# Low-rank products of a recurrence on half of the array each: a two-layer transformer block on one Trainium2 core

## The chip, the cores and the metric

The kernel runs on one core of a Trainium2 chip. The metric is the device time of one execution in microseconds (us), and the comparison is the median of several executions of each kernel. The core's engines have queues of their own and run in order: PE (TensorE, matmuls; PEld is its weight load), DVE (VectorE), ACT (ScalarE), POOL (GpSimd) and SP (SyncE, which issues most transfers).

## The reference

The function computes two layers on 256 tokens of width 2048 in fp32. The change touches the recurrence of the first layer, an RWKV-7 time mix with 16 heads of 64, of which this is the part that matters here (`heads` splits 1024 columns into heads; the scan and the norm behind it are left out):

```python
def rwkv7_time_mix(p_r, p_k, p_v, p_wd, p_ad, ...):
    ...
    wd = token_shift_lerp(p_wd, f(mu_w))          # 64 wide
    ad = token_shift_lerp(p_ad, f(mu_a))          # 64 wide
    w = -jax.nn.softplus(-(f(w0) + jnp.tanh(wd) @ f(w2))) - 0.5
    decay = jnp.exp(-jnp.exp(w))
    a = jax.nn.sigmoid(f(a0) + ad @ f(a2))
    kk = heads(k * f(k_k))
    kk = kk * lax.rsqrt(jnp.maximum(jnp.sum(kk * kk, axis=-1, keepdims=True), 1e-24))
    k = k * (1.0 + (a - 1.0) * f(k_a))
    ...
    o = rwkv7_scan(rh, dh, kh, vh, -kk, kk * ah)
```

The two low-rank products are `tanh(wd) @ w2`, for the decay, and `ad @ a2`, for the gate `a`. Each contracts over 64.

## The kernel before

Activations are held as 128 rows by tokens. Every large weight arrives in pieces of 128x1024 (SP), is cut into a rounded part `wh` by ACT (L171) and a rest `wl` by DVE (L179) or, for 7 pieces in 10 of the recurrence's stage, by POOL in four quarters (L177), and goes through PE as pairs of matmuls into a bank `g` of PSUM (three of them): 512 columns with `wh`, 256 with `wl`. Such a product is evicted by ACT (`et`, L220) and DVE (`z`, L223).

The recurrence runs in eight pairs of heads. For pair p there are three steps. `rwkv_inputs(p)` makes k, r and v by three large products, then the decay and the gate by the low-rank products, from these `kk`, `k`, and the tiles `atrt`, `bt_d`, `kt_d` that everything after it reads; `k`, `r`, `v`, `s`, `a`, `kk`, `bt_d`, `kt_d` and `t0` (the low-rank weights first, then the square of kk, which the matmul into `pk` sums) have one buffer each, so the next pair's inputs wait until this pair's are used up. `rwkv_inverse(p)` reads them by twelve matmuls into `G` (L593 to L595), and inverts a triangular matrix by five rounds of `Z` and `D`, each a matmul, a DVE instruction and the next matmul. `rwkv_chain(p)` walks over four chunks: a matmul, a copy by DVE (`X`), a matmul, a copy (`U`), a matmul, the new state by DVE (`S`), and so on; these matmuls write `ch` and `oT`.

The loop over p writes chain(p), inverse(p+1), inputs(p+2) and then fillers: group products of attention (`A0` to `A5`), gates, attention heads, and gate products of the merge that are made ahead and put into DRAM (L745). The order in which each engine gets its instructions is not that of the source: a scheduler sets it when the program is built, from its own estimate of times, and keeps it fixed. It may only move what the buffers allow. PSUM has eight banks in this stage: three for `g`, one for the tag `s` (pl, pk, ptk, sc of the attention over tokens), two for the tag `z` (G, Z and D of the inverse, among others), one for `ch` and one for `oT`. A tile of a tag gets the next bank of that tag in the order of the source, and has to wait until the tile that had it before is used up.

Behind the last pair, `raw` is cut into `yhl` (24 times an ACT cast, L234, and a DVE subtraction, L235), and `merge` reads it.

The lines that the change touches are in `rwkv_inputs`: `lora` holds tanh(wd) in rows 0 to 63 and ad in rows 64 to 127; `w2` is a tile whose columns 0 to 127 hold w2 in rows 0 to 63 and zeros below, and whose columns 128 to 255 hold zeros above and a2 in rows 64 to 127. Both products contract over all 128 rows and write the two halves of one bank, `pl`, of the tag `s`.

Of the kernel before, what the change touches and what calls it, by code (L numbers as in the profile page):

```python
# [11 lines left out]
AF = mybir.ActivationFunctionType  # L12
# [88 lines left out]
def _body(tc, a, out):  # L101
    nc = tc.nc
# [26 lines left out]
    def P(n, j=0, w=1):  # L129
        o, _ = _P[n]  # L130
        return par[:, o + j:o + j + w]

    def C(n, j=0, w=None):
        o, ww = _C[n]
        return con[:, o + j:o + j + (ww - j if w is None else w)]
# [10 lines left out]
    def ps_small(name, tag="s"):  # L146
        return psp.get(tag, psp["s"]).tile([128, 512], F32, tag=tag if tag in psp else "s", name=name)
# [4 lines left out]
    def mm(dst, lhsT, rhs, start=True, stop=True):  # L152
        nc.tensor.matmul(dst, lhsT=lhsT, rhs=rhs, start=start, stop=stop)  # L153
# [28 lines left out]
    def gemm_B(wd, act, kt=KD, m=128):  # L182

        ps = psg.tile([128, 512], F32, tag="g", name="g")
        for k0, kn in (chunks(kt) if m == 128 else [(0, kt)]):
            src = wd[128 * k0 * m:128 * (k0 + kn) * m].rearrange("(p c) -> p c", p=128)
            wh, wl = wchunk(src, kn * m)
            for j in range(kn):
                k = k0 + j
                mm(ps[:m, :], wh[:, j * m:(j + 1) * m], act[:, k, :], start=(k == 0), stop=False)  # L190
                mm(ps[:m, 256:512], wl[:, j * m:(j + 1) * m], act[:, k, 0:256], start=False, stop=(k == kt - 1))
        return ps
# [25 lines left out]
    def evict(ps, m=128, rstd=None, out=None, name="z"):  # L218
        t = scr.tile([128, 256], F32, tag="et", name="et", bufs=2)
        nc.scalar.copy(t[:m], ps[:m, 256:512])  # L220
        if rstd is None:
            z = out if out is not None else scr.tile([128, 256], F32, tag="ez", name=name, bufs=3)
            nc.vector.tensor_add(z[:m], ps[:m, 0:256], t[:m])  # L223
            return z
        nc.vector.tensor_add(t[:m], ps[:m, 0:256], t[:m])
        z = out if out is not None else scr.tile([128, 256], F32, tag="ez", name=name, bufs=3)
        nc.vector.tensor_mul(z[:m], t[:m], rstd[:m])
        return z
# [25 lines left out]
    def rsqrt(u, y):  # L254

        nc.scalar.activation(y, u, AF.Sqrt)
        nc.vector.reciprocal(y, y)  # L257
        newton(u, y)
# [82 lines left out]
    if True:  # L341
# [80 lines left out]
        hw0 = const.tile([128, 16], F32, tag="hw0", name="hw0")  # L422
        nc.vector.tensor_scalar(hw0, P("w0", 0, 16), 0.5, None, op0=ALU.mult)

        def shift(dst, z, mu):

            t = rw.tile([128, 256], F32, tag="tA", name="tA")
            nc.vector.tensor_sub(t, z[:, 0:256], z[:, 1:257])
            nc.vector.scalar_tensor_tensor(dst, t, mu, z[:, 1:257], op0=ALU.mult, op1=ALU.add)
# [59 lines left out]
        def raw_tile(ps):  # L489
            z = rw.tile([128, 257], F32, tag="zr", name="zr", bufs=2)  # L490
            nc.gpsimd.memset(z[:, 0:1], 0.0)
            evict(ps, out=z[:, 1:257])
            return z

        zw = raw_tile(gemm_B(a["w1B"][0], xg))
        lora = rw.tile([128, 256], F32, tag="lora", name="lora")
# [14 lines left out]
        def c4(t):  # L511
            return t.rearrange("p (c t) -> p c t", c=4)

        def diag(dst, off, fn):
            for h in range(2):
                s = slice(64 * h, 64 * h + 64)
                fn(dst[s, :, off + 64 * h:off + 64 * h + 64], s)

        def tmp(tag, bufs=1, shape=(128, 256), dt=F32):
            return rw.tile(list(shape), dt, tag=tag, name=tag, bufs=bufs)  # L520
# [3 lines left out]
        def rwkv_inputs(p):  # L524

            k = tmp("k")
            shift(k, raw_tile(gemm_B(a["w1B"][1 + p], xg)), P("mu_k", p))
            r = tmp("r")
            shift(r, raw_tile(gemm_B(a["w1B"][9 + p], xg)), P("mu_r", p))
            v = tmp("v")  # L530
            shift(v, raw_tile(gemm_B(a["w1B"][17 + p], xg)), P("mu_v", p))
            w2 = tmp("t0")
            nc.sync.dma_start(w2, a["lora2"][p])
            pl = ps_small("pl")
            mm(pl[:, 0:256], w2[:, 0:128], lora)
            mm(pl[:, 256:512], w2[:, 128:256], lora)
            s = tmp("s")
            nc.scalar.activation(s, pl[:, 0:256], AF.Tanh, bias=hw0[:, p:p + 1], scale=0.5)
            av_ = tmp("a")
            nc.scalar.activation(av_, pl[:, 256:512], AF.Tanh, bias=hw0[:, 8 + p:9 + p], scale=0.5)  # L540
            nc.vector.tensor_scalar(s, s, 0.5, 0.5, op0=ALU.mult, op1=ALU.add)
            nc.vector.tensor_scalar(av_, av_, 0.5, 0.5, op0=ALU.mult, op1=ALU.add)
            cum = tmp("cum")
            nc.vector.tensor_tensor_scan(cum, C("scan"), s, 0.0, op0=ALU.mult, op1=ALU.add)
            nc.gpsimd.tensor_sub(s, cum, s)
            e1 = s
            nc.scalar.activation(e1, s, AF.Exp, scale=-DECAY_C)
            ep = tmp("ep", 2)
            nc.scalar.activation(ep, cum, AF.Exp, scale=-DECAY_C)
            en = cum  # L550
            nc.scalar.activation(en, cum, AF.Exp, scale=DECAY_C)

            kk = tmp("kk")
            nc.vector.tensor_scalar(kk, k, P("k_k", p), None, op0=ALU.mult)
            t0 = tmp("t0")
            nc.scalar.activation(t0, kk, AF.Square)
            pk = ps_small("pk")
            mm(pk[:, 0:256], bdones, t0)
            nc.vector.tensor_scalar(t0, pk[:, 0:256], 1e-24, None, op0=ALU.max)
            rsqrt(t0, tmp("tA"))  # L560
            nc.vector.tensor_mul(kk, kk, t0)

            nc.vector.tensor_scalar(t0, av_, -1.0, P("k_a", p), op0=ALU.add, op1=ALU.mult)
            nc.vector.scalar_tensor_tensor(k, t0, 1.0, k, op0=ALU.add, op1=ALU.mult)

            nc.vector.scalar_tensor_tensor(t0, r, P("r_k", p), k, op0=ALU.mult, op1=ALU.mult)
            mm(pk[:, 256:512], bdones, t0)
            nc.vector.tensor_mul(raw[:, 8 + p, :], v, pk[:, 256:512])

            atrt = atrt_b[p % 2]  # L570
            diag(atrt, 64, lambda d, sl: nc.vector.scalar_tensor_tensor(
                d, c4(kk)[sl], -1.0, c4(e1)[sl], op0=ALU.mult, op1=ALU.mult))
            nc.vector.tensor_mul(atrt[:, :, 0:64], c4(r), c4(ep))
            nc.gpsimd.tensor_mul(kk, kk, av_)
            diag(bt_d, 0, lambda d, sl: nc.vector.tensor_mul(d, c4(kk)[sl], c4(en)[sl]))
            diag(kt_d, 0, lambda d, sl: nc.vector.tensor_mul(d, c4(k)[sl], c4(en)[sl]))
            diag(v_d, 0, lambda d, sl: nc.gpsimd.tensor_copy(d, c4(v)[sl]))

            pair[p] = dict(atrt=atrt, ep=ep)
# [206 lines left out]
        def filler(p):  # L786
            for f in fillers[p]:
# [6 lines left out]
                else:  # L794
                    (group_A if f[0] == "A" else attention_A)(int(f[1]))

        rwkv_inputs(0)
        group_C()
        rwkv_inverse(0)
        attention_C_prep()  # L800
        attention_C(0)
        attention_C(1)
        rwkv_inputs(1)
        ahead(0)
        ahead(1)
        for p in range(8):
            rwkv_chain(p)
            if p == 0:
                attention_C(2)
                attention_C(3)  # L810

                r16b = r16p.tile([128, 4096], F32, tag="r16", name="r16b")
                aqk = r16b[:, 0:2048].rearrange("p (i t f) -> p i t f", i=2, t=2)
                tok_b.append(r16b[:, 2048:3584].rearrange("p (i c f) -> p i c f", i=3, c=4))
            if p < 7:
                rwkv_inverse(p + 1)
            if p < 6:
                rwkv_inputs(p + 2)
            filler(p)
# [94 lines left out]
    for i in range(8):  # L914
        z = evict(gemm_B(a["w2B"][i], xg2), rstd=rs_bc)
# [8 lines left out]
    for h in range(4):  # L924
# [7 lines left out]
        z = evict(gemm_B(a["w2B"][8 + h], xg2), rstd=rs_bc)  # L932
        nc.vector.scalar_tensor_tensor(qi, z, 128.0 ** -0.5, eq, op0=ALU.mult, op1=ALU.mult)
        ki = atp.tile([128, 256], F32, tag="ki", name="ki")
        z = evict(gemm_B(a["w2B"][12 + h], xg2), rstd=rs_bc)
# [10 lines left out]
        pa = ps_small("pa")  # L946
# [88 lines left out]
    for f in range(KF):  # L1035
        z = evict(gemm_B(a["w_gate"][f], xg3), rstd=rs_bc)
# [9 lines left out]
    p = ps_small("fin")  # L1046
# [92 lines left out]
```

## Time and profile before

| | us |
|---|---|
| median of 3 executions | 2959.39 |
| lowest and highest | 2958.73, 2959.72 |
| the profiled execution | 2959.55 |
| its span, first to last instruction | 2957.8 |
| PE busy in the span | 2919.8 |
| DVE busy | 1917.6 |
| ACT busy | 1452.8 |
| POOL busy | 645.9 |

A view by windows gives, for each stretch of the span, the busy time of each engine with the number of its instructions, and the share of TensorE's full clock that was granted (PEclk: 1.00 is 2.4 GHz, 0.50 is 1.2 GHz). A timeline row gives the start, the time, the engine, the line and the tiles, with the idle time of the engine ahead of it in brackets and who ended it. Matmuls overlap, so what one costs in a stream is the distance of starts, not its time. An fp32 matmul stands as two instructions in the trace.

### The profile page before, as it was taken

Reading aid. Unit: us, or ns where it says so; the run is one execution under the profiler, and the core shown is the slowest. Engines: PE = TensorE matmul, PEld = TensorE weight load, DVE = VectorE, ACT = ScalarE, POOL = GpSimd, SP = SyncE. Lnnn points to the kernel's source line nnn. Section 1 sums busy time; section 2 is a strip of 40 time slices with the busy share of each in tenths; the row PEclk is TensorE's granted clock in tenths of the full one; section 3 lists DMA queues with packets and bytes.
Section 4 is the critical chain, followed back from the end, with each engine's and each line's share of the span. In section 5 each row is a group of like instructions: output and inputs, shape, how many; then the busy total and the mean of one; then the engine's idle time right before and its main releaser. Section 6 shows DMA issues by size and latency. Waiting matters only on the chain.

```text
span 2957.8 us, 44491 instructions
## 1 busy us (share of the span) xinstructions
PE 2919.8 (99%) x16696; PEld 2567.0 (87%) x16696; DVE 1917.6 (65%) x3088; ACT 1452.8 (49%) x2201; POOL 645.9 (22%) x878
## 2 busy tenths in 40 slices
PE   9999999999999999999999999999999999999997
PEld 7888888889988888888888888888888888888886
DVE  6655776677637655657767766666667666666554
ACT  6443454445446554545454454454555444444443
POOL 0685577767683100100000000000000000000000
PEclk9999999999999999999999999999999999999999
DMA  7553344444456655655455555555555555555664
GB/s 285 181 173 104 109 133 144 141 137 134 132 171 206 208 190 192 210 179 178 143 174 170 191 191 188 191 191 188 191 186 192 190 189 191 191 188 188 189 189 146
DMA packets 150392, 522.45 MB, mean 177 GB/s; under 512 B 17104, under 2 KB 22480, under 8 KB 150176
## 3 DMA queue, kind: packets, MB, share of 16 engines
q1 hardware_dynamic: 147920, 513.47, 53.1%
q0 software_dynamic: 1824, 4.98, 0.4%
q8 instruction: 131, 2.15, 0.3%
q10 hardware_dynamic: 432, 1.15, 0.1%
q14 instruction: 85, 0.70, 0.1%
HBM read 514.56 MB, written 4.98 MB: 176 GB/s over the span
## 4 chain that ended last, share of the span: by engine, by line
PE 94%; DVE 4%; ACT 1%; POOL 1%; issue 0%; DMA 0%; DVEq 0%; SPq 0%; ACTq 0%; POOLq 0%
PE g L153 87%; PE D L153 1%; PE ch L153 1%; PE Z L153 1%; PE oT L153 1%; PE sc L153 1%; PE G L153 1%; PE po L153 1%; POOL wl L177 0%; DVE wl L179 0%; PE ptk L150 0%; PE glo L153 0%; PE pt L150 0%; PE pl L153 0%; DVE tA L257 0%
## 5 line engine op out<-in xcount | busy, mean ns | idle before, releaser
L153 PE MATMUL g<-xg,wh 128*128 128x512 f32 x4640 | 1633.7, 393 | 0.5 <-DVE z L223 0.5
L171 ACT CAST wh<-w 128x1024 fp32r<-128x1024 f32 (+1 forms) x962 | 1002.3, 1042 | 1253.9 <-PE g L153 760.2
L179 DVE TENSOR_TENSOR wl<-w,wh 128x1024 fp32r<-128x1024 f32 (+1 forms) x801 | 977.1, 1220 | 712.7 <-ACT wh L171 711.6
L153 PE MATMUL g<-xg,wl 128*128 128x256 f32 x4640 | 1317.8, 284 | 4.9 <-POOL wl L177 4.6
L153 PEld LDWEIGHTS g<-xg,wh 128*128 128x128 f32 x4640 | 871.0, 188 | 178.2 <-DVE z L223 0.7
L153 PEld LDWEIGHTS g<-xg,wl 128*128 128x128 f32 x4640 | 876.4, 189 | 7.5 <-POOL wl L177 4.9
L177 POOL TENSOR_TENSOR wl<-w,wh 128x256 fp32r<-128x256 f32 x644 | 494.9, 801 | 164.0 <-ACT wh L171 149.4
L153 PE MATMUL g<-yhl,wh 128*128 128x512 f32 x768 | 269.7, 390 | 0.0
L153 PE MATMUL g<-act,wh 128*128 128x512 f32 x704 | 244.2, 390 | 0.0
L153 PE MATMUL g<-wh,xg 128*128 128x512 f32 x768 | 243.7, 401 | 0.4 <-ACT va L357 0.4
L153 PE MATMUL g<-yhl,wl 128*128 128x256 f32 x768 | 216.6, 282 | 0.0
L153 PE MATMUL g<-act,wl 128*128 128x256 f32 x704 | 198.7, 282 | 0.0
L848 POOL TENSOR_TENSOR accm<-accm,z 128x256 f32<-128x256 f32 x64 | 53.4, 834 | 651.0 <-DVE z L847 651.0
L153 PEld LDWEIGHTS g<-yhl,wh 128*128 128x128 f32 x768 | 144.2, 188 | 30.4 <-ACT wh L171 0.3
L153 PEld LDWEIGHTS g<-wh,xg 128*128 128x128 f32 x768 | 142.4, 188 | 31.0 <-ACT va L357 0.5
L220 ACT COPY et<-g 128x256 f32<-128x256 f32 (+1 forms) x434 | 157.2, 362 | 6.9 <-PE g L153 6.9
L153 PEld LDWEIGHTS g<-act,wh 128*128 128x128 f32 x704 | 132.2, 188 | 27.7
L153 PE MATMUL g<-wl,xg 128*128 128x512 f32 x384 | 149.8, 404 | 0.2 <-DVE wl L179 0.2
L153 PEld LDWEIGHTS g<-yhl,wl 128*128 128x128 f32 x768 | 145.1, 189 | 0.0
L153 PEld LDWEIGHTS g<-act,wl 128*128 128x128 f32 x704 | 133.1, 189 | 0.0
L223 DVE TENSOR_TENSOR z<-g,et 128x256 f32<-128x256 f32 x216 | 90.3, 418 | 31.4 <-ACT et L220 31.1
L1010 POOL MEMSET cu<- 128x2 f32 x8 | 0.8, 102 | 415.1 <-DVE co L1017 350.3
(369 smaller groups left out, 2950.0 us busy)
## 6 DMA issues: line engine op xcount, KB each, us to landing
w<-w2B SPq DMA_DIRECT2D x208, 512.0 KB, 3.3
w<-w1B SPq DMA_DIRECT2D x194, 512.0 KB, 3.4
w<-w_gate SPq DMA_DIRECT2D x88, 512.0 KB, 3.3
w<-w_ffup SPq DMA_DIRECT2D x88, 512.0 KB, 3.3
w<-w1A SPq DMA_DIRECT2D x64, 512.0 KB, 3.3
w<-w_down SPq DMA_DIRECT2D x64, 448.0 KB, 3.3
w<-w_o SPq DMA_DIRECT2D x32, 512.0 KB, 4.3
w<-w2A SPq DMA_DIRECT2D x32, 512.0 KB, 3.4
```

Of the source, the lines that this page charges most:

```text
L153: nc.tensor.matmul(dst, lhsT=lhsT, rhs=rhs, start=start, stop=stop)
L171: nc.scalar.copy(wh[:, :nel], w[:, :nel])
L177: nc.gpsimd.tensor_sub(wl[:, sl], w[:, sl], wh[:, sl].bitcast(F32))
L179: nc.vector.tensor_sub(wl[:, :nel], w[:, :nel], wh[:, :nel].bitcast(F32))
L220: nc.scalar.copy(t[:m], ps[:m, 256:512])
L223: nc.vector.tensor_add(z[:m], ps[:m, 0:256], t[:m])
L848: nc.gpsimd.tensor_add(accm, accm, u)
L1010: nc.gpsimd.memset(cu[:, 0:2], 0.0)
```

## The change

The first product reads rows 0 to 63 of the weights and of `lora`, the second rows 64 to 127; the zeros are not read any more. In the built program the first has the place (0, 0) in an array of 64 rows by 128 columns, the second (64, 0). The second writes a bank of its own, `pa`, and that comes from the tag `z`, so it takes its turn among the tiles of the inverse. ACT reads the gate from there. All else in the source is as it was, and since the scheduler runs anew on it, the order of all engines differs from there to the first products of the merge.

```diff
@@ -531,13 +531,14 @@
             shift(v, raw_tile(gemm_B(a["w1B"][17 + p], xg)), P("mu_v", p))
             w2 = tmp("t0")
             nc.sync.dma_start(w2, a["lora2"][p])
-            pl = ps_small("pl")
-            mm(pl[:, 0:256], w2[:, 0:128], lora)
-            mm(pl[:, 256:512], w2[:, 128:256], lora)
+
+            pl, pa = ps_small("pl"), ps_small("pa", "z")
+            mm(pl[:, 0:256], w2[0:64, 0:128], lora[0:64, :])
+            mm(pa[:, 0:256], w2[64:128, 128:256], lora[64:128, :])
             s = tmp("s")
             nc.scalar.activation(s, pl[:, 0:256], AF.Tanh, bias=hw0[:, p:p + 1], scale=0.5)
             av_ = tmp("a")
-            nc.scalar.activation(av_, pl[:, 256:512], AF.Tanh, bias=hw0[:, 8 + p:9 + p], scale=0.5)
+            nc.scalar.activation(av_, pa[:, 0:256], AF.Tanh, bias=hw0[:, 8 + p:9 + p], scale=0.5)
             nc.vector.tensor_scalar(s, s, 0.5, 0.5, op0=ALU.mult, op1=ALU.add)
             nc.vector.tensor_scalar(av_, av_, 0.5, 0.5, op0=ALU.mult, op1=ALU.add)
```

Lines behind it have a number higher by one. Three places show what the scheduler made of it. The first is PE's queue at the low-rank products of pair 0, as a piece of the difference (`g` are the large products, `wh` and `wl` the weight's parts, `xg` the activations, `t_1159` the tile of the low-rank weights):

```order
 L153 MATMUL g<-xg,wh 128x512
 L153 MATMUL g<-xg,wl 128x256
-L153 MATMUL pl<-lora,t_1159 128x256 x2
+L153 MATMUL pl<-lora,t_1159 128x256
+L153 MATMUL pa<-lora,t_1159 128x256
 L153 MATMUL g<-wh,xg 128x512 x2
 L153 MATMUL g<-wl,xg 128x512
```

The two products still stand side by side there; it is the only pair of the eight in which they do.

The second place is PE's queue at the products of pair 5 (`t_4906` before, `t_4911` now). Before:

```order
L153 MATMUL D<-tt,Z 128x128
L153 MATMUL oT<-gm,r16b 128x64
L153 MATMUL pl<-lora,t_4906 128x256 x2
L153 MATMUL g<-wh,xg 128x512 x2
L153 MATMUL g<-wl,xg 128x512
L153 MATMUL g<-wh,xg 128x512 x2
```

Now, around the gate's product, with the chain of pair 4 (`ch`, `oT`) and `pk`, the norm of pair 5's kk, behind it:

```order
L153 MATMUL Z<-Z,tt 128x128 x4
L153 MATMUL pa<-lora,t_4911 128x256
L153 MATMUL ch<-X,ttf 128x128
L153 MATMUL ch<-btok 128x128
L153 MATMUL ch<-U,btok 128x128
L153 MATMUL oT<-gm,U 128x64
L153 MATMUL pk<-t_4932,con 128x256
L153 MATMUL ch<-S,atrt_975 128x128
L153 MATMUL ch<-btok,gm 128x128
L153 MATMUL oT<-atrt_975,S 128x64
L153 MATMUL oT<-gm,btok 128x64
L153 MATMUL ch<-X,ttf 128x128
```

The gate's product has moved behind the last `Z` of the inverse ahead of it, and the chain's steps, which had large products between them, follow each other directly; the decay's product stands 193 rows earlier.

The third place is DVE's queue at the end of the recurrence's stage: the last lines of pair 7's norm, the last gate (L740 before, L741 now), and `yhl`. Before:

```order
L694 TENSOR_TENSOR oT<-oT,gq 128x256
L695 TENSOR_SCALAR oT<-oT,par 128x256
L179 TENSOR_TENSOR wl<-w,wh 128x1024
L223 TENSOR_TENSOR z<-g,et 128x256
L740 SCALAR_TENSOR_TENSOR raw<-z,raw 128x256
L235 TENSOR_TENSOR yhl<-raw,yhl 128x256 x21
L223 TENSOR_TENSOR z<-g,et 128x256
L235 TENSOR_TENSOR yhl<-raw,yhl 128x256 x2
L179 TENSOR_TENSOR wl<-w,wh 128x1024
L235 TENSOR_TENSOR yhl<-raw,yhl 128x256
```

Now:

```order
L695 TENSOR_TENSOR oT<-oT,gq 128x256
L696 TENSOR_SCALAR oT<-oT,par 128x256
L179 TENSOR_TENSOR wl<-w,wh 128x1024
L223 TENSOR_TENSOR z<-g,et 128x256
L741 SCALAR_TENSOR_TENSOR raw<-z,raw 128x256
L235 TENSOR_TENSOR yhl<-raw,yhl 128x256 x24
L179 TENSOR_TENSOR wl<-w,wh 128x1024
L223 TENSOR_TENSOR z<-g,et 128x256
```

The 24 subtractions stand in one piece now, and in PE's queue 51 large matmuls stand between the last fp32 matmul of pair 7's norm and the first that reads `yhl`, where 110 stood.

## Rows read from the trace of the kernel before

**Rows 1.** The page: span, then each engine's busy time, share and instructions.
```profile
span 2957.8 us, 44491 instructions
PE 2919.8 (99%) x16696; PEld 2567.0 (87%) x16696; DVE 1917.6 (65%) x3088; ACT 1452.8 (49%) x2201; POOL 645.9 (22%) x878
```

**Rows 2.** Waits of PE over the span: total us, times, longest.
```profile
PE g L153 <- POOL wl L177: 4.6, 1, 4.6
PE ch L153 <- DVE U L665: 2.6, 3, 1.4
```

**Rows 3.** Windows: stretch and length; PE, PEld, DVE, ACT, POOL busy (instructions); PEclk; DMA.
```profile
100.00:900.00 800.00, 788.54 (x4656) 695.08 (x4654) 520.79 (x1031) 374.35 (x578) 567.89 (x767) 0.99 0.43 140
900.00:2940.00 2040.00, 2036.42 (x11644) 1796.65 (x11645) 1324.63 (x1932) 1009.82 (x1516) 71.78 (x97) 1.00 0.57 187
268.40:274.60 6.20, 4.97 (x19) 4.01 (x19) 6.03 (x17) 0.00 (x0) 1.94 (x3) 0.50 0.07 21
274.60:278.40 3.80, 3.80 (x11) 3.08 (x11) 1.50 (x6) 0.00 (x0) 0.73 (x2) 0.50 0.00 0
276.00:400.00 124.00, 120.05 (x709) 105.12 (x708) 95.46 (x193) 58.07 (x91) 69.89 (x99) 0.99 0.32 105
```

**Rows 4.** The tile pl: durations in ns, shortest, median, longest; first and last start.
```profile
L153 PEld LDWEIGHTS pl<-lora,t x32: 188/190/192, 123.4 to 666.6; 128*128 128x128 f32 x32
L153 PE MATMUL pl<-lora,t x32: 377/379/435, 123.6 to 666.9; 128*128 128x256 f32 x32
```

**Rows 5.** Timeline of PE around the products of pair 0.
```profile
123.21 0.39 PE L153 MATMUL g<-xg,wh 128*128 128x512 f32 x1
123.44 0.28 PE L153 MATMUL g<-xg,wl 128*128 128x256 f32 x1
123.56 1.03 PE L153 MATMUL pl<-lora,t 128*128 128x256 f32 x4
124.23 0.81 PE L153 MATMUL g<-wh,xg 128*128 128x512 f32 x2
124.88 0.40 PE L153 MATMUL g<-wl,xg 128*128 128x512 f32 x1
```

**Rows 6.** Timeline of PE through the chain of pair 0.
```profile
266.69 0.44 PE L153 MATMUL ch<-X,ttf 128*128 128x128 f32 x2
267.60 0.49 PE L153 MATMUL ch<-btok 128*128 128x128 f32 x2 [0.47 <-DVE U L665]
267.92 0.39 PE L153 MATMUL ch<-U,btok 128*128 128x128 f32 x2
268.14 0.36 PE L153 MATMUL oT<-gm,U 128*128 128x64 f32 x2
268.98 0.80 PE L153 MATMUL ch<-S,atrt 128*128 128x128 f32 x2 [0.48 <-DVE S L672]
...
273.30 0.80 PE L153 MATMUL ch<-btok 128*128 128x128 f32 x2 [0.75 <-DVE U L665]
...
274.63 1.59 PE L153 MATMUL sc<-kT,qT 128*128 128x256 f32 x3
```

**Rows 7.** Timeline of pair 1's inputs from pk to bt_d, there.
```profile
261.29 0.59 PE L153 MATMUL pk<-t,con 128*128 128x256 f32 x2
...
264.06 1.75 DVE L257 RECIPROCAL tA<-tA 128x256 f32<-128x256 f32 x1 [1.71 <-ACT tA L256]
272.07 0.85 DVE L575 TENSOR_TENSOR bt_d<-kk,cum 64x256 f32<-64x256 f32 x2
```

**Rows 8.** The end of the stage: timeline rows, and L235 as a group.
```profile
881.70 0.42 DVE L692 TENSOR_SCALAR gq<-oT 128x256 f32<-128x256 f32 x1 [2.40 <-PE oT L153]
892.14 0.43 DVE L740 SCALAR_TENSOR_TENSOR raw<-z,raw 128x256 f32<-128x256 f32 x1 [0.30 <-POOL raw L696]
897.99 6.87 POOL L177 TENSOR_TENSOR wl<-w,wh 128x256 fp32r<-128x256 f32 x3 [2.46 <-ACT wh L171]
L235 DVE TENSOR_TENSOR yhl<-raw,yhl 128x256 fp32r<-128x256 f32 x24 | 12.5, 586 | 0.0
```

## The prediction

> **What bounds the kernel now.** I read the page's first part, then the waits of PE, then windows over the stages, and then the timeline where PE waits. PE is busy 2919.8 of 2957.8 us, and no other engine reaches two thirds [rows 1]. So the time is PE's work plus what PE waits. Its waits are few and have places [rows 2]: from 900 us on it is idle 3.6 us in 2040, while in the first layer's recurrence, from 100 to 900 us, 11.5 us are idle [rows 3]. There the reader should look at two stretches. From 266.7 to 274.6 us PE walks the chain of pair 0 with no large product in between, and each step waits for a copy by DVE [rows 6]. At 898 us three quarters of a weight's rest took POOL 6.87 us, and PE waited 4.6 us for them [rows 2, 8]. The granted clock falls behind such stretches: it is 0.50, which is 1.2 GHz, from 268.4 to 278.4 us, beginning inside the chain and lasting 3.8 us beyond it, though PE is busy all of those [rows 3].
>
> **The products themselves.** The 32 instructions of pl have a median of 0.38 us [rows 4], and in the stream the four of a pair cost less: from 123.56 to 124.88 us stand these four and two wide matmuls; a wide one is 0.23 us (123.21 to 123.44), so four cost 0.86 us, and one product 0.43 [rows 5]. Eight pairs are 6.9 us of PE. An instruction's length goes by its columns here (a narrow g starts the next after 0.12, a wide one after 0.23 [rows 5]), and those stay at 256, so reading 64 rows saves nothing by itself. The gain can come only from two products that run at once in the two halves, and for that they must stand next to each other. In the built queue they do so in pair 0 alone. That is -0.43 us, between 0 and -0.43.
>
> **The change between whole and half arrays.** The products stand in 15 places now, so the array's form changes 30 times. No row shows one. The cheapest is nothing; the dearest is an empty pipe and a load that nothing hides: 0.38 less the 0.215 of a start to the next, and 0.19 for the load [rows 4, 5], 0.35 in all, or 10.6 us. The nearest row is the entry from g into pl, which costs nothing that I can see [rows 5]; I take 0.05 each, 1.5 us.
> The Trainium skill ("TensorEngine Tiling (Array Packing)", Key Properties) speaks against this change: going from one tiling mode to another drains the engine. By that rule, each change would cost the emptying of the pipe, 0.16 us by rows 4 and 5, and the term would be 4.9 us rather than 1.5.
>
> **What moves, and this decides.** pa takes a bank of the tag z, in turn behind the inverse of the pair before. So PE can't start the gate's product before the last Z of that inverse, and the gate is needed for k, kk, bt_d and kt_d, which the next inverse reads first. The square of kk, which pk sums, takes the buffer of the low-rank weights (both are t0), so pk too waits until pa has read them. Counted in PE's work, by the durations above, the products of pair 3 stood 55 us ahead of that pair's first G and those of pair 5 about 100 us; now the gate's product stands 6 and 4 us ahead of it. The next pair's k, r and v can't take its place, since their tiles have one buffer and are in use until then, and the three banks of g are given out in the order of the source, so the fillers behind them are held up too. The queue shows the outcome: PE has nothing left to put between the chain's steps.
>
> I went through PE's rows of both programs and added, for each matmul that reads what DVE or ACT made of an earlier one, the PE work that stands between the two. Before, under 1.0 us of it stands in a few places around the chain of pair 0 alone, and these remain, alike in number. New are 27 round trips: in the chain of pair 2 beside the gate of pair 3 five; one Z in the inverse behind it; around the gate of pair 5 ten (two steps of Z and D, the last of them, and seven of the chain of pair 4); and eleven in the inverse of pair 5, among the attention heads h4 to h7. Of these, 16 have under 0.3 us of work between, 11 have 0.5 to 1.0.
>
> *Price of a round trip.* From 266.69 to 274.63 us are 7.94 us with four of them (X to U, U to S, S to X, X to U). PE's work in it is eight ch at 0.22 (267.92 to 268.14), four oT of half the columns at 0.11, and one pk at 0.43, so 2.6 us; 5.3 are lost [rows 6]. From 268.4 us on the clock is half [rows 3], which doubles 1.9 us of that work. 3.4 are left, 0.85 per trip. 16 x 0.85 = 13.6; for the other 11 I take half, 4.4; together 18.0. The ends: the idle time alone that the rows show, 0.47 [rows 6], for 16 trips only, 7.5; and 1.3 for 16 and 0.9 for 11, 30.7.
>
> *Clock.* Each of the two long bare stretches (pairs 3 and 5) should set it to 1.2 GHz as there: 1.9 us inside, and half of the 3.8 us behind [rows 3], 3.8 in all, 7.6 for two. Ends: none, and three times half of the whole 10 us, 15.
>
> *The way from pk to G.* In both stretches pk, the norm of kk, stands 3.4 us of work ahead of the first matmul that reads bt_d. Between these lie a square root, a reciprocal of 1.75 us, and more: from pk at 261.29 to bt_d's end at 272.92 us are 11.6 us [rows 7]. The bare trips and the half clock in the same stretch fill most of that. I add 1.5 us each, 3.0, between 0 and 9.2.
>
> *What goes away.* From 276 to 400 us 4.0 us were idle, in places that the new order doesn't have [rows 3]; I take half of it, -2.0.
>
> *The end of the stage.* From DVE's first line behind the last norm's matmul, 881.70, to the last gate at 892.14 are 10.4 us, and 0.9 more to the first piece of yhl [rows 8]. PE now has 51 large matmuls for it, at 0.175 on average 8.9 us: a wait of 2.4. Then yhl comes every 0.52 us (12.5 for 24 [rows 8]) where PE reads one in 0.35: 4.1. Then the next weight's rest stands behind the whole train, 1.2. That is 7.7. POOL's last pieces now stand ahead of its last add to raw, so the wait of 4.6 [rows 2] goes: +3, between -5 and +6.
>
> Costed at nothing: the four more table loads of ACT, which is 49% busy [rows 1], and the eight transfers of the low-rank weights, which move by up to some ten places in SP's queue; the decay's product, the first that needs them, has large products around it. If that cover were gone, pl and ACT's work behind it would be late, and with them the same G, so the way from pk to G bounds it.
>
> **The sum.** 18.0 + 7.6 + 3.0 - 2.0 + 3.0 + 1.5 - 0.4 = 30.7. The profiled execution is 2959.55 us (its span is 1.75 less, and the median of the runs 0.16 less), so 2990. All lower ends give 2958, all upper ends 3031; both need every term at once.
>
> **Rivals.** A measurement of this kernel can tell about 0.2%, 5.9 us, from no change.
> *Trips almost for nothing* (0.12): DVE is free in the bare stretches and answers at 0.47, the clock doesn't fall, the 4.0 idle us go: 7.5 - 4.0 - 0.4, so 2963. For it speaks that only the idle time in rows 6 is named as a wait; against it that 5.3 us were lost there.
> *The late POOL pieces decide* (0.05): the wait of 4.6 at the stage's end goes and none takes its place, because the last norm runs faster than before; with 0.4 and 2.0 from above that is 2952.5. It decides only if everything else costs under 1 us, where the order has 27 bare steps.
> *Side by side after all* (0.02): the two halves run at once in all eight pairs, 8 x 0.43, so 2956. Against it, 14 of the 16 products stand alone.
> The Trainium skill ("TensorE: Matmul & The Clock Gate", Part 3, on packing small matmuls) states that products in different rows of the array run concurrently, starting about 4 ns apart; it is this rival, and it needs products in sequence, which the queue has once.
> *The clock stays down* (0.13): the eleven trips among the attention heads set it back three times more, 11.4, and changes of form cost 0.35: 30.7 + 11.4 + 9.1, so 3011.
>
> **The numbers.** The forecast holds 0.68. Slower by over 0.2% is it and the clock case: 0.81. Within 0.2% are the first and the third rival: 0.14. Faster by more: 0.05. The range goes from 2962, which takes in the first rival, to 3013, with the last one in it; outside lie the fast cases and the tails of my own.
>
> **What would show it.** In the trace of the changed kernel, pl should be one block of about 0.45 us in pair 0 and single products of 0.43 elsewhere. PE's waits for X, U, S, Z and D should add up to some 20 us more, most of it in two stretches around 400 and 550 us, each with PEclk 0.50 for some 10 us. G should wait for bt_d or kt_d behind both. The wait for POOL's wl should be gone, with one for yhl in its place. I am wrong if large matmuls run in those stretches without a wait, or if the time is lost at the products themselves.

## The result: 45.9 us slower

The changed kernel takes 3005.61 us (median of 5 runs, 3005.10 to 3006.34), the kernel before 2959.72 us beside it (5 runs, 2958.73 to 2960.08). The ratio is 1.0156, with a 95% interval of 1.0145 to 1.0167. The prediction said 2990.0, between 2962 and 3013: the sign, the range and the main mechanism held, and 15 us of the loss were missing from the sum. One execution of experiment e5 below (3206.17 us at a granted clock of 0.848) fell into a slower state of the chip and is left out of its median.

The page of the changed kernel, as [rows 1] of before:

```profile
span 3003.7 us, 44526 instructions
...
PE 2945.3 (98%) x16696; PEld 2579.3 (86%) x16696; DVE 1915.5 (64%) x3088; ACT 1459.8 (49%) x2205; POOL 630.1 (21%) x878
```

The span grew by 45.9 us. PE has the same 16696 matmuls, yet is busy 25.5 us longer (2945.3 against 2919.8) and idle 20.4 us longer (58.4 against 38.0). These are two different losses, and each has a view of its own. The idle part first: the waits of PE over the span, as [rows 2].

```profile
...
PE ch L153 <- DVE U L666: 5.1, 5, 2.2
PE pk L153 <- DVE t L567: 3.9, 3, 3.1
PE g L153 <- DVE yhl L235: 3.9, 1, 3.9
PE G L153 <- DVE bt_d L576: 2.4, 4, 1.4
PE pt L150 <- DVE tp L717: 2.2, 2, 1.1
...
PE G L153 <- DVE kt_d L577: 1.8, 4, 0.7
```

POOL's `wl` (4.6 before) is gone from the list, and the wait for `yhl` has come in its place. Added over all rows of this view, the waits of the chain's and the inverse's matmuls (`ch`, `oT`, `Z`, `D`) went from 7.0 to 14.2 us, those of `G` from 0.6 to 4.2, those of `pk` from 1.4 to 3.9. Steps of attention and transposes that had no wait before (`pt`, `po`, `ptk`, `tra`) have 6.3.

The largest share of the busy part is the clock. Windows of the changed kernel, as [rows 3]: the recurrence's stage, then every stretch ahead of the last 20 us in which the granted clock is half.

```profile
100.00:900.00 800.00, 768.85 (x4382) 666.85 (x4381) 499.97 (x982) 353.00 (x526) 531.37 (x723) 0.97 0.40 131
...
266.70:276.90 10.20, 8.05 (x29) 6.60 (x28) 9.66 (x24) 0.00 (x0) 4.51 (x9) 0.50 0.18 64
294.00:297.40 3.40, 3.01 (x11) 2.57 (x11) 3.07 (x9) 0.42 (x1) 0.00 (x0) 0.50 0.51 154
369.10:372.50 3.40, 3.23 (x12) 3.13 (x13) 3.37 (x7) 0.37 (x1) 2.04 (x4) 0.50 0.48 155
444.20:454.40 10.20, 8.45 (x29) 7.46 (x30) 9.29 (x26) 0.37 (x1) 1.61 (x4) 0.50 0.23 66
604.60:618.30 13.70, 11.79 (x43) 10.35 (x43) 10.71 (x27) 2.19 (x4) 2.76 (x5) 0.50 0.14 48
645.60:649.00 3.40, 3.40 (x12) 3.01 (x13) 3.12 (x10) 0.98 (x4) 0.93 (x3) 0.50 0.69 222
952.80:959.60 6.80, 6.02 (x19) 5.18 (x20) 6.80 (x21) 6.77 (x19) 0.56 (x1) 0.50 0.43 134
```

The engine stands at 1.2 GHz for 51.1 us now; PE is busy 44.0 us of these, and if the same work took half at 2.4 GHz, 22.0 us are lost. In the kernel before, such stretches hold 13.6 us (the chain of pair 0 [rows 3], and the one below) with 12.4 of work, 6.2 lost.

```profile
903.20:906.60 3.40, 3.40 (x11) 2.92 (x12) 3.40 (x4) 0.00 (x0) 3.40 (x4) 0.50 0.00 0
```

The difference is 15.8 us of the 25.5, and that is an upper bound: a bare step of the chain takes 0.80 us at 1.2 GHz and 0.49 at 2.4 (rows below), and a wide and a narrow large matmul together 0.64 and 0.35, so less than half goes back. By the bare step's ratio for all of it, the difference is 12.3. Each stretch stands at bare steps of a chain or an inverse, at the waits of `G` for `kt_d` and `bt_d` (369 us), or behind the wait for `yhl`. In the stage from 100 to 900 us PE is idle 31.2 us, where 11.5 were idle before.

The longest wait between two steps of a chain is new, and it stands at pair 3's gate. PE there:

```profile
437.17 0.70 PE L153 MATMUL pa<-lora,t 64*128 64x256 f32 x2
...
442.00 0.49 PE L153 MATMUL ch<-X,ttf 128*128 128x128 f32 x2
444.70 0.80 PE L153 MATMUL ch<-btok 128*128 128x128 f32 x2 [2.21 <-DVE U L666]
...
450.26 1.22 PE L153 MATMUL pk<-t,con 128*128 128x256 f32 x2 [0.49 <-DVE t L567]
451.27 1.49 PE L153 MATMUL G<-atrt,kt_d 128*128 128x192 f32 x4
```

And DVE in the same stretch:

```profile
442.74 1.75 DVE L257 RECIPROCAL tA<-tA 128x256 f32<-128x256 f32 x1 [0.80 <-ACT tA L256]
444.41 0.23 DVE L666 COPY U<-ch 128x128 f32<-128x128 f32 x1
...
450.12 0.84 DVE L577 TENSOR_TENSOR kt_d<-k,cum 64x256 f32<-64x256 f32 x2
451.00 0.85 DVE L576 TENSOR_TENSOR bt_d<-kk,cum 64x256 f32<-64x256 f32 x2
```

The gate comes at 437.17, and all of pair 3's inputs that hang on it (by its value, or by the buffer `t0`) run on DVE in the same microseconds in which the chain of pair 2 asks DVE for a copy at each step. `ch<-X` started at 442.00, but its copy `U` stands in DVE's queue behind a reciprocal of 1.75 us and starts at 444.41. A round trip is not only bare: its middle stands in a queue with the very work that the late gate has pushed there.

The products themselves, at pair 0, as [rows 5]:

```profile
122.77 0.28 PE L153 MATMUL g<-xg,wl 128*128 128x256 f32 x1
122.98 0.48 PE L153 MATMUL pl<-lora,t 64*128 64x256 f32 x1
122.98 0.48 PE L153 MATMUL pa<-lora,t 64*128 64x256 f32 x1
123.30 0.38 PE L153 MATMUL pl<-lora,t 64*128 64x256 f32 x1
123.30 0.38 PE L153 MATMUL pa<-lora,t 64*128 64x256 f32 x1
```

The two halves do run at once. But the second pass of an fp32 product starts 0.32 us behind the first, where a whole one takes about 0.215, and the first starts 0.21 behind the narrow `g` instead of 0.12.

### The profile page after: what moved, and what is told of

Read it like the earlier page. It is cut to its first block, busy times and chain, and to the rows that moved or that the text cites. A ratio compares the mean times of both kernels' runs of the same rounds, so it can differ in the third digit from the quotient of the medians.

```text
span 3003.7 us, 44526 instructions
## 1 busy us (share of the span) xinstructions
PE 2945.3 (98%) x16696; PEld 2579.3 (86%) x16696; DVE 1915.5 (64%) x3088; ACT 1459.8 (49%) x2205; POOL 630.1 (21%) x878
## 4 chain that ended last, share of the span: by engine, by line
PE 93%; DVE 5%; ACT 1%; issue 1%; POOL 0%; DMA 0%; DVEq 0%; SPq 0%; ACTq 0%; POOLq 0%
PE g L153 86%; PE D L153 1%; PE ch L153 1%; PE G L153 1%; PE Z L153 1%; PE sc L153 1%; PE oT L153 1%; PE po L153 0%; DVE tA L257 0%; DVE wl L179 0%; PE ptk L150 0%; ACT wh L171 0%; PE glo L153 0%; DVE atrt L572 0%; DVE kt_d L577 0%
## 5 line engine op out<-in xcount | busy, mean ns | idle before, releaser
L177 POOL TENSOR_TENSOR wl<-w,wh 128x256 fp32r<-128x256 f32 x644 | 485.6, 786 | 205.0 <-ACT wh L171 190.3
L849 POOL TENSOR_TENSOR accm<-accm,z 128x256 f32<-128x256 f32 x64 | 47.2, 737 | 665.2 <-DVE z L848 665.2
L153 PE MATMUL g<-mg,wh 128*128 128x512 f32 x256 | 88.7, 390 | 0.0
```

Of the source, the lines that this page charges most:

```text
L177: nc.gpsimd.tensor_sub(wl[:, sl], w[:, sl], wh[:, sl].bitcast(F32))
L849: nc.gpsimd.tensor_add(accm, accm, u)
```

## The experiments

The theory on record was: the loss comes from pa's turn in the tag `z` (and from the weights' buffer `t0`, which pa holds until then), not from the half arrays. The rivals were the half arrays themselves, with a drain at each change of form, and the second bank as such. In all runs below the kernel before took 2959.0 to 2959.4 us on the same chip.

**Whole products, bank turn kept** (e1). Against the changed kernel:

```diff
             pl, pa = ps_small("pl"), ps_small("pa", "z")
-            mm(pl[:, 0:256], w2[0:64, 0:128], lora[0:64, :])
-            mm(pa[:, 0:256], w2[64:128, 128:256], lora[64:128, :])
+            mm(pl[:, 0:256], w2[:, 0:128], lora)
+            mm(pa[:, 0:256], w2[:, 128:256], lora)
```

> Both products over all 128 rows again, but still each in a bank of its own, the gate's in a bank of the tag z: only the half arrays are undone. The built order is that of the changed kernel but for 117 of PE's 16148 places. If the bank's place in the turn makes the loss, as the prediction has it, the time stays near the changed kernel's 3005.6: the 14 lone products should give back some 0.25 us each and the pair of pair 0 lose 0.2, so 3002, between 2998 and 3006. If the half arrays make the loss, it falls to 2960 to 2965.

Measured: 2999.67 us, ratio to before 1.0135 (1.0118 to 1.0152). PE's order is that of the changed kernel but for 117 of 16148 places. So 40.4 us of the loss stay without any half array, and the half arrays make 5.9 (5.5, if each kernel is taken against the kernel before beside it).

**The gate's product in a bank of `g`**, half (e2) and whole (e3). Against the changed kernel, e2 is the first line alone:

```diff
-            pl, pa = ps_small("pl"), ps_small("pa", "z")
+            pl, pa = ps_small("pl"), psg.tile([128, 512], F32, tag="g", name="pa")
...
-            mm(pl[:, 0:256], w2[0:64, 0:128], lora[0:64, :])
-            mm(pa[:, 0:256], w2[64:128, 128:256], lora[64:128, :])
+            mm(pl[:, 0:256], w2[:, 0:128], lora)
+            mm(pa[:, 0:256], w2[:, 128:256], lora)
```

> The half products stay, but the gate's bank comes from the three of the large products instead of the tag z, so it need not wait for the inverse. Counted as in the prediction, 4 bare round trips are left beyond the first chain instead of 29. If the turn in z makes the loss, the time is 2958 to 2970; if half arrays do, it stays above 2995.

> As the run before with the gate's bank among those of the large products, but both products over all 128 rows; the built order is the same place by place. The difference of the two is the price of the half arrays alone: 10 lone products at some 0.25 us more and three pairs at 0.2 less make the half form slower by 1.9 us, between 0 and 4. If halves paid as they were meant to, it would be faster by 1 to 3.

Measured: e2 2971.77 us, 1.0044 (1.0029 to 1.0059), 1.8 above the range that the theory gave it; e3 2968.27 us, 1.0030 (1.0018 to 1.0042). With two banks for the two products, and the second from `g`, 9.0 us of loss are left; most of the loss goes by whose turn the second bank takes. With whole products, taking it from `g` instead of `z` is worth 31.4 us (e1 less e3). The order of e2 and e3 is the same to the last row, so their difference, 3.5 us, is the half arrays alone: ten lone products in e2 and three pairs side by side (by the prices of e8 below it would be 3.8). The side-by-side pairs gain next to nothing: from the narrow `g` ahead to the third `g` behind are 1.41 us with halves (660.40 to 661.81 in e2) and 1.44 with whole ones (655.13 to 656.57 in e3).

**One bank, whole products, but from `z`** (e4). Against the kernel before:

```diff
-            pl = ps_small("pl")
+            pl = ps_small("pl", "z")
```

> The kernel before, with both whole products in one bank as there, but that bank from the tag z. No half array, no second bank. 29 bare round trips are counted in its order. If the turn in z alone makes the loss, 2995 to 3008; if it needs the split into two banks, or the halves, 2960 to 2970.

Measured: 3006.01 us, 1.0156 (1.0141 to 1.0172). A turn in `z`, without half arrays and without a second bank, makes a loss of the same size, 46.8 us. That the sizes agree so closely is in part luck, since here the decay's product is late too, and the half arrays' share is not in it. The waits of PE in e4:

```profile
PE pk L153 <- DVE t L566: 10.8, 5, 3.3
PE g L153 <- DVE yhl L235: 8.7, 1, 8.7
...
PE ch L153 <- DVE X L662: 3.9, 3, 2.0
```

The places differ from the changed kernel's: with both products behind the inverse, the second matmul into `pk`, the sum over r, k and `r_k` that stands ahead of `G`, waits five times, up to 3.3 us, for its input (L566). The kind is the same, small matmuls that wait for DVE. PE is idle 69.1 us here and stands at 1.2 GHz for 41.0, so the same time as in the changed kernel is made of more idle time and less of the clock.

**The shared buffer** (e5). e1, with one line more:

```diff
-            w2 = tmp("t0")
+            w2 = scr.tile([128, 256], F32, tag="sq", name="w2", bufs=3)
```

> The first experiment (whole products, the gate's bank from the tag z) with one thing more: the low-rank weights get a buffer of another tag, so the square of kk, and with it pk, no longer waits until the gate's product has read them. In its order 14 bare round trips are left of 30, three of them under 0.45 us. If the shared buffer t0 carries a good part of the loss, 2976 to 2990 (16 trips at 0.85 and half of the slow clock, some 18 us, below 2999.7); if the bank's turn alone decides, it stays above 2995.

Measured: 2978.11 us, 1.0063 (1.0046 to 1.0080), 21.6 us less than e1. By the prediction's way of counting, 14 bare steps are left in its order, where e1 has 30. Its page:

```profile
span 2973.8 us, 44538 instructions
...
PE 2926.4 (98%) x16696; PEld 2572.1 (86%) x16696; DVE 1928.3 (65%) x3088; ACT 1458.5 (49%) x2205; POOL 640.4 (22%) x878
```

PE is idle 47.4 us (61.0 in e1) and busy 10.7 us less. So about half of what the turn costs came through `t0`: as long as pa had not read the weights, the square of kk had no place to go. The new buffer also reorders other work, so the 21.6 us hold for the two changes of order together.

**Both products in one bank of `g`** (e6): before, with `pl = psg.tile([128, 512], F32, tag="g", name="pl")`.

> The kernel before with both whole products in one bank, as there, but that bank from the three of the large products. In its order no bare round trip is left behind the chain of pair 0, which has its 8 as before. By the count of bare trips 2955 to 2963; if taking a bank from the large products costs by itself, as it may have in the run with two banks (2968.3), 2964 to 2972.

Measured: 2975.08 us, 1.0052 (1.0035 to 1.0068). This is a miss. My count finds no new bare step in that order, and 15.6 us are lost all the same. The longest wait is in PE's timeline at the end of the stage:

```profile
896.02 0.39 PE L153 MATMUL g<-xg,wh 128*128 128x512 f32 x1
903.96 0.80 PE L153 MATMUL g<-xg,wh 128*128 128x512 f32 x1 [7.55 <-ACT wh L171]
904.55 0.41 PE L153 MATMUL g<-xg,wl 128*128 128x256 f32 x1
```

A large product waits 7.55 us for its weight's cast by ACT, and runs at half the clock behind it (0.80 for a wide matmul instead of 0.39). ACT in turn waited for DVE, and one of DVE's subtractions for `yhl`, 0.41 us right behind it, took 8.91 us beside twelve of POOL's quarters of `wl`:

```profile
890.83 8.91 DVE L235 TENSOR_TENSOR yhl<-raw,yhl 128x256 fp32r<-128x256 f32 x1
...
891.14 8.31 POOL L177 TENSOR_TENSOR wl<-w,wh 128x256 fp32r<-128x256 f32 x12
...
901.12 0.42 ACT L731 ACTIVATE et<-z 128x256 f32<-128x256 f32 x1 [7.30 <-DVE z L223]
```

In the kernel before, 4.6 us of waiting for POOL stood at the end of the stage, and 1.7 of such waits are left here, so the net loss in idle time there is some 4.7. Attention steps between 230 and 262 us wait 4.3 more, and the engine is at 1.2 GHz for 30.7 us instead of 13.6. The count looks only at matmuls that read what DVE or ACT made of another matmul; a large product that is fed late is not in it.

**A mixed version** (e7): whole products, one bank, tag `s` for pairs 0 and 1 and `g` for the rest, and `w2` in `sq`.

```diff
-            w2 = tmp("t0")
+            w2 = scr.tile([128, 256], F32, tag="sq", name="w2", bufs=3)
...
-            pl = ps_small("pl")
+            pl = ps_small("pl") if p < 2 else psg.tile([128, 512], F32, tag="g", name="pl")
```

> Whole products in one bank: from the tag s for pairs 0 and 1, as before, from those of the large products for pairs 2 to 7; and the low-rank weights in a buffer of another tag. One bare trip more than in the kernel before is counted, but the chain of pair 0 starts 17 us earlier in PE's work. 2953 to 2964; under 2955 it would beat the kernel before.

Measured: 2961.03 us, 1.0008 (0.9999 to 1.0018). It doesn't beat the kernel before.

**The price of a half product** (e8). Idle fp32 products of 256 columns stand behind each gate product of the feed-forward network, where PE never waits; four kinds take turns, and nobody reads their result:

```diff
         z = evict(gemm_B(a["w_gate"][f], xg3), rstd=rs_bc)
+        pm, pn = ps_small("pm"), ps_small("pn")
+        if f % 4 == 0:
+            mm(pm[:, 0:256], ident, xr[:, 0, :])
+        elif f % 4 == 1:
+            mm(pm[:, 0:256], ident[64:128, :], xr[64:128, 0, :])
+        elif f % 4 == 2:
+            mm(pm[:, 0:256], ident[0:64, :], xr[0:64, 0, :])
+            mm(pn[:, 0:256], ident[64:128, :], xr[64:128, 0, :])
...
```

> The kernel before with idle fp32 products of 256 columns put between the large products of the feed-forward layer, whose results nobody reads; 44 places, four kinds in turn: one whole, one half (rows 64 to 127), two halves side by side in two banks, two of the same half in two banks. By the traces so far a whole one adds 0.43 us to PE's stream, a lone half 0.82, two halves side by side 0.83, and two of the same half, if a load can't hide behind the product in its own half, about 1.4. If halves are cheap, a lone half would add 0.43 to 0.5 and two side by side 0.5. In all some 11 x 3.5 = 38 us more than before.

Measured: 3000.66 us in one execution, 41.2 above before. Three stretches of PE's timeline, a whole product first, then a lone half, then two halves:

```profile
2502.88 0.28 PE L153 MATMUL g<-xg,wl 128*128 128x256 f32 x1
2502.99 0.59 PE L153 MATMUL pm<-xr,con 128*128 128x256 f32 x2
2503.23 0.58 PE L153 MATMUL g<-xg,wh 128*128 128x512 f32 x1
2503.66 0.28 PE L153 MATMUL g<-xg,wl 128*128 128x256 f32 x1
```

```profile
2487.47 0.39 PE L153 MATMUL g<-xg,wh 128*128 128x512 f32 x1
2487.79 0.70 PE L153 MATMUL pm<-xr,con 64*128 64x256 f32 x2
2488.41 0.38 PE L153 MATMUL g<-xg,wl 128*128 128x256 f32 x1
2488.64 0.40 PE L153 MATMUL g<-xg,wh 128*128 128x512 f32 x1
```

```profile
2478.19 0.28 PE L153 MATMUL g<-xg,wl 128*128 128x256 f32 x1
2478.40 0.48 PE L153 MATMUL pm<-xr,con 64*128 64x256 f32 x1
2478.40 0.48 PE L153 MATMUL pn<-xr,con 64*128 64x256 f32 x1
2478.72 0.38 PE L153 MATMUL pm<-xr,con 64*128 64x256 f32 x1
2478.72 0.38 PE L153 MATMUL pn<-xr,con 64*128 64x256 f32 x1
2479.03 0.50 PE L153 MATMUL g<-xg,wh 128*128 128x512 f32 x1
2479.37 0.28 PE L153 MATMUL g<-xg,wl 128*128 128x256 f32 x1
```

In each, the first and the last row stand a narrow and a wide `g` apart, 0.345 us in the stream. What is above that is the product's cost: 0.78, 1.17 and 1.18 less 0.345 are 0.435, 0.825 and 0.835. Over all places, each within 3 ns of the others, it is 0.436 for a whole product (10 places), 0.829 for a lone half (32) and 0.837 for two halves side by side (11); one place with a whole and a half next to each other has 1.249. These add up to 41.3, where 41.2 were measured. So a lone half costs 0.39 more than a whole product, and two halves at once save 0.035 against two whole ones. The two products of the fourth kind, both in the same half, stand apart in the built order, so they count as lone ones, and what they cost next to each other was not measured.

**The buffer without the turn** (e9): the kernel before with the line of e5 alone.

> Before, with only w2 of delta_chunks moved from the shared t0 buffers to a buffer of the tag sq. If the shared buffer costs only where the low-rank products share a bank tag in turn (theory: its delay is hidden as long as pl takes its banks as before), the time is that of before, 2959 us, within 2953 to 2964. If the buffer already lengthens chains in before, the time falls below 2950 us.

Measured: 2960.01 us, 1.0004 (0.9995 to 1.0013). The shared buffer costs nothing as long as pl takes its banks from `s`. No version that was run is faster than the kernel before.

## Why the prediction was right, and where it was not

**What decides** held. The prediction named the turn in `z`, and with it `t0`. e4 makes the loss with the turn alone, e3 takes most of it back by another turn, e5 half of it by another buffer, and e9 shows that the buffer costs nothing without the turn. But for e2 and e3, and nearly so the changed kernel and e1, no two versions have the same order: each was scheduled anew, so what is measured is a turn together with the order that the scheduler made of it.

**The sum** has a slip: half of 0.85 for 11 trips is 4.7 and not 4.4, so it should be 31.0 instead of 30.7. The time lies nearer to the rival in which the clock stays down (3011) than to the forecast (2990).

**The idle time** was right in sum and not in its places, and that is luck. Round trips, the way from pk to G, the idle time that goes, and the end of the stage were 22.0 together; PE's idle time grew by 20.4. By the waits, the chain and the inverse make 7.2 of it, against 18.0 for the round trips. In the three places where the 27 trips stand the waits add up to 8.5 us, 0.31 each; the price of 0.85 was all time lost in a chain that walks alone, of which [rows 6] shows 0.47 to 0.75 as idle. DVE was not free to answer either, as pair 3's reciprocal shows. The way from pk to G has 3.6 more as waits of `G` for `bt_d` and `kt_d`, where 3.0 was said, but none of it at pairs 3 and 5, for which it was said. The second matmul into `pk` stands on the same way, right ahead of `G`, and waits 2.5 us more than before, so the way made 6.1. Most of that is at 538.23 us, where the matmul stands between large products and halts them for 3.1 us. There the instruction that it waits for took 3.30 us itself, where its shortest takes 0.49, and ended 0.3 us behind a train of POOL's quarters:

```profile
534.88 3.30 DVE L567 SCALAR_TENSOR_TENSOR t<-r,par,k 128x256 f32<-128x256 f32 x1
...
535.13 2.76 POOL L177 TENSOR_TENSOR wl<-w,wh 128x256 fp32r<-128x256 f32 x4
```

e4 has the same at 533.33 us (3.31 beside four quarters). The prediction has no term for DVE and POOL holding each other up; it read such a hold in [rows 8], POOL's 6.87 us beside the train of `yhl` on DVE, as POOL's own time. No run moved POOL's work away. Outside the sum, too, attention steps and transposes wait 6.3. The 27 bare steps are a good sign of trouble and a poor price list: e6 has none new and loses 15.6, and e4 with 29 waits most at `pk`.

**The clock** was the term that was sized worst: 7.6 forecast, 12.3 to 15.8 by the windows. The two stretches that were named, pairs 3 and 5, are there, at 444 and 605 us, with up to 4.2 and 5.9 lost (half of 8.45 and 11.79) where 3.8 each was said. Three short ones at 294, 369 and 646 us lose up to 4.8 more. The prediction had these only as a rival, with a chance of 0.13, and put them behind the attention heads; the first two stand beside the chains of pairs 0 and 1. And the wait for `yhl` brings 3.0 where 903.2 to 906.6 lost 1.7 before. This split holds for the profiled execution alone. Its granted clock is 0.989 over the span, that of two others 0.991, some 10 us less at 1.2 GHz, and these took 0.1 us more and 0.4 us less. So the clock's part is not a price that simply adds to the waits: a slower PE may wait less for DVE. That is argued, since the waits of those two executions are not on record.

**The end of the stage**: the wait of 4.6 for POOL went and one of 3.9 for `yhl` came, as forecast; with the clock behind both it is +0.6 rather than +3.0.

**The change of form** was 1.5 for 30 changes, at 0.05 each, since the entry into pl showed no cost in [rows 5]. That row shows an entry without a change of form, so it spoke for nothing. Fourteen lone products at 0.39 are 5.5, and e1 has 5.5 to 5.9. That is 0.2 per change, inside the bounds of 0 to 0.35 and four times the value taken.
The Trainium skill's rule ("TensorEngine Tiling (Array Packing)", Key Properties), that a change of tiling mode drains the engine, was the reason for the other size of this term, 4.9, and e1 and e8 agree with that better than with my reading.
In e8 the second pass inside the product is late as well (0.32 behind the first instead of 0.215), which is no change of form.

**Side by side**: I took -0.43 for the pair that stands together. The halves start 6 to 8 ns apart in e8, so they do run at once, yet the pair saves 0.035, so this term was all but zero. The rows of e8 show where the gain goes: the first pass starts 0.1 us late, each of the two passes takes about 0.32, and the second large matmul behind them comes another 0.1 late.
The Trainium skill ("TensorE: Matmul & The Clock Gate", Part 3) gives about 4 ns between such starts, and the trace, with its 6 to 8 ns, agrees with that in kind.
So the rival of 2956, with all eight pairs side by side, could not have come true either: 8 x 0.035 is 0.3 us.

In one line, us: idle 20.4, clock 15.8 at most, lone half products 5.5, which is 41.7 of 45.9. The other 4.2, or up to 7.7 with the clock at 12.3, is busy time of PE that I have not separated; matmuls of bare steps, which stand alone, may be a part of it. Against the forecast of 30.7, the 15.2 us that were missing are the clock (up to 8.2), the lone half products (4.0), the pair that gained nothing (0.4) and this rest, less 1.6 of idle time. That the holes cause the low clock is read from their places in the trace; no run changed the one without the other.

## What to carry to other kernels

When a tile moves to another tag, ask whose turn it now waits for, and which buffers it holds until then: in a kernel whose big matmuls fill the gaps of a recurrence, that turn was worth 40 us, and the arithmetic that the edit was about was worth 6 us, the wrong way. Here, reading half the rows of an fp32 product of 256 columns saved nothing, and a lone half product in a stream of whole ones cost nearly twice a whole one; zeros in the unused half were the cheaper way. Where a bare chain shares DVE with the work that its late input releases, price both, and the clock behind it, from the stretch of the trace that looks most alike; and where a short DVE instruction takes microseconds, look at what POOL does beside it.

## What the runs showed of the hardware that was not expected

- A lone half-array fp32 product of 256 columns between whole ones: 0.829 us of the stream against 0.436; its two passes are 0.32 us apart, and the next whole product's weight load starts only together with its matmul (both at 2488.41 us in e8), where a whole product's load starts a matmul ahead.
- Two such products in different halves and banks start 6 to 8 ns apart, and cost 0.837 together.
- A DVE instruction of 128x256 can stand through a train of POOL's quarters of `wl` and end 0.3 us behind it: 8.91 us beside twelve quarters (e6, L235, 0.41 right behind it), 5.52 beside eight (e4, L261 at 523.75, median 0.42), 3.30 beside four (the changed kernel, L567, shortest 0.49). Others of that size beside such quarters (529.5 to 533.4 us in the changed kernel) took under 1 us; what decides which is held, no run shows. It goes the other way too: in the kernel before, one quarter took 5.13 us (897.99 to 903.12, mean of all 0.80) beside a train of subtractions for `yhl`, and that is part of the 4.6 us for which PE waited.
- At 1.2 GHz a wide matmul and a narrow one take 0.64 us together (954.35 to 954.99 in the changed kernel) instead of 0.35, though PE has no wait there: the granted clock, not the list of waits, shows that loss.
